# Starts and pass orders that change from column tile to column tile, and three load buffers, in a two-layer decoder trunk

## The chip, the cores and the metric

The kernel runs on one core of a Trainium2 chip. The metric is the time of one execution of the whole program on the device, in microseconds (us). TensorE (PE in the profile) does the matrix products and has two rows there: PE for the matmuls and PEld for the loads of their stationary operand, which overlap them. VectorE is DVE, ScalarE is ACT, GpSimd is POOL, SyncE is SP; SP only issues transfers here.

## What is computed

The input is one sequence of 256 tokens with 1024 features. Two layers follow, and a last norm. Each layer has a half-step SwiGLU, a mixer (a Mamba-2 scan in layer 0, sliding-window attention in layer 1) and another half-step SwiGLU. All is float32.

```python
D_MODEL, SEQ, D_FF = 1024, 256, 2816

def swiglu(h, w_gate, w_up, w_down):
    return (jax.nn.silu(h @ w_gate) * (h @ w_up)) @ w_down

for layer in range(2):
    if layer == 1:
        k_shared, v_shared = shared_kv(x, kv_norm_w, w_k, b_k, w_v, b_v, cos, sin)
    x = x + 0.5 * swiglu(rmsnorm(x, norm_w[layer, 0]), w_gate[layer, 0], w_up[layer, 0], w_down[layer, 0])
    h = rmsnorm(x, norm_w[layer, 1])
    x = x + (mamba2_mixer(h, ...) if layer == 0 else swa_sink_attention(h, k_shared, v_shared, ...))
    x = x + 0.5 * swiglu(rmsnorm(x, norm_w[layer, 2]), w_gate[layer, 1], w_up[layer, 1], w_down[layer, 1])
return rmsnorm(x, final_norm_w)
```

## The kernel before, in words

The activations lie transposed: 8 tiles of 128 features by 256 tokens. Every float32 product is made of three passes of the float32r type: an operand is cut into a rounded high part and the rest, the low part, and the kernel adds high x high, high x low and low x high. The activations' parts stand side by side in `xs` (columns 0 to 255 high, called `xh`; 256 to 511 low, called `xl`). Weights come in units of 128 x 1024; there are 341, in the order that `order()` writes out. A load brings two units (1 MB) into a buffer `raw`, of which there are `RAW`. For each unit ScalarE rounds the high part into a tile `hi` (L144) and VectorE makes the low part `lo` (L155), with six buffers each, four to five units ahead of TensorE. When the second unit of a buffer is cut, `low` issues the next load (L134).

The four SwiGLUs are named (l, i): (0, 0) and (0, 1) in layer 0, (1, 0) and (1, 1) in layer 1. Each goes over 22 column tiles f of 128 hidden features. A tile takes three units: `g` and `u` (gate and up, in `wide`) and, four tiles later, `d` (down, in `rows`). `wide` runs 8 matmuls of 512 columns with `hi` against all of `xs`, and 8 of 256 columns with `lo` against `xh`. They alternate for each k, or, with `by_part`, the 8 wide ones come first and then the 8 narrow ones. `evac` makes the SwiGLU's result and cuts it into `hh` and `hl`, of six buffers each in the pool `op`. `rows` runs 24 matmuls of 256 columns, three for each of 8 output tiles: hi x hh, lo x hh, hi x hl, or with `high_first` hi x hh, hi x hl, lo x hh. Before the change `by_part` (for f > 0) and `high_first` are on where l differs from i, that is in (0, 1) and (1, 0). The output projections of the mixers (`so` in the scan, `ao` in attention) use `rows` without `high_first`. The other units (`dt`, `B`, `C`, `x`, `z`, `qA`, `qB`, `kA`, `kB`) use `unit`: 24 matmuls of 256 columns. The scan and the attention also have small float32 matmuls between units.

The order on each engine is as the code is written; `Slots` only says after which unit a piece of evacuation is issued. A home (the buffer of a tile) is 4096 bytes a partition for `hi` and `lo` and 1024 bytes for `hh` and `hl`, so all homes of a pool start at one place modulo 512 bytes. In the built program that is 160 for `hi`, `lo` and for the key and value operands `xkh` and `xkl`, and 480 for `xs`, `hh` and `hl`.

Of the kernel before, what the change touches and what calls it, by code (L numbers as in the profile page):

```python
# [10 lines left out]
F32R = mybir.dt.float32r  # L11
# [5 lines left out]
P = 128  # L17
T = 256
D = 1024
KT = D // P  # L20
# [11 lines left out]
GROUPS = 4  # L32
EPS = 1e-5
CH = 2
RAW = 4
NEG = -1.0e30


def ffn_order(l, i):
# [32 lines left out]
def order():  # L72
    return ffn_order(0, 0) + ssm_order() + ffn_order(0, 1) + ffn_order(1, 0) + att_order() + ffn_order(1, 1)


ORDER = order()
# [33 lines left out]
class Weights:  # L110
# [27 lines left out]
    def high(self, half=None):  # L138
        u = self.rounded
        c, i = divmod(u, CH)  # L140
        if not half:
            self.hi = self.parts.tile([P, D], F32R, tag="hi", name=f"hi{u}")
        hi, s = self.hi, self.piece(half)
        self.nc.scalar.activation(hi[:, s], self.chunks[c][:, i, s], AF.Copy)  # L144
        if half != 0:
            self.ready[u] = hi
            self.rounded += 1

    def low(self, half=None):
        u = self.cut  # L150
        c, i = divmod(u, CH)
        if not half:
            self.lo = self.parts.tile([P, D], F32R, tag="lo", name=f"lo{u}")
        hi, lo, s = self.ready.get(u, self.hi), self.lo, self.piece(half)
        self.nc.vector.tensor_tensor(lo[:, s], self.chunks[c][:, i, s], hi[:, s].bitcast(F32), ALU.subtract)  # L155
        if half == 0:
            return
        self.ready[u] = (hi, lo)
        self.cut += 1
        if i == CH - 1 or u == NU - 1:  # L160
            del self.chunks[c]
            self.load()

    @staticmethod
    def piece(half):
# [20 lines left out]
class Slots:  # L186
# [11 lines left out]
    def at(self, d, *fs):  # L198
        self.put(d, 0, fs)
# [16 lines left out]
class Trunk:  # L216
    def __init__(self, ctx, tc, a):
# [7 lines left out]
        self.wk = ctx.enter_context(tc.tile_pool(name="work", bufs=2))  # L225
        raw = ctx.enter_context(tc.tile_pool(name="raw", bufs=RAW))
        parts = ctx.enter_context(tc.tile_pool(name="parts", bufs=self.NPART))
# [37 lines left out]
        nc.sync.dma_start(self.sm, a["small"])  # L265
        for _ in range(RAW - 3):
            self.W.load()
# [86 lines left out]
    def wide(self, what, out, by_part=False):  # L354


        hi, lo = self.W.next(what)
        passes = [(k, w, x, n) for k in range(KT) for w, x, n in ((hi, self.xs, 2 * T), (lo, self.xh, T))]
        if by_part:
            passes = passes[0::2] + passes[1::2]  # L360
        for n, (k, w, x, c) in enumerate(passes):
            self.nc.tensor.matmul(  # L362
                out[:, 0:c], w[:, k * P : (k + 1) * P], x[k],
                start=n == 0, stop=n == len(passes) - 1, skip_group_check=True,
            )
        self.tick()
# [2 lines left out]
        self.slots.run()  # L369
        self.W.ahead(self.NPART - 2)  # L370

    def rows(self, units, accs, first, last, done=None, high_first=False):

        nc = self.nc
        for j in range(KT):
            out = accs[j % 4][:, (j // 4) * T : (j // 4) * T + T]
            s = slice(j * P, (j + 1) * P)
            for n, ((hi, lo), hh, hl) in enumerate(units):
                f, e = first and n == 0, last and n == len(units) - 1
                passes = ((hi, hh), (hi, hl), (lo, hh)) if high_first else ((hi, hh), (lo, hh), (hi, hl))  # L380
                for m, (w, x) in enumerate(passes):
                    nc.tensor.matmul(  # L382
                        out, w[:, s], x, start=f and j < 4 and m == 0, stop=e and m == 2, skip_group_check=True
                    )
            if done:
                done(j, out)
# [90 lines left out]
    def ffn(self, l, i, key, nxt):  # L477
        nc, wk = self.nc, self.fw
        self.stage_norm(key)
        accs = self.accs(f"da_{key}")  # L480
        hs = {}

        def evac(f, g, u):
            hh = self.op.tile([P, T], F32R, tag="high", name=f"hh_{key}_{f}")
            hl = self.op.tile([P, T], F32R, tag="low", name=f"hl_{key}_{f}")
            hs[f] = (hh, hl)

            def e0():
                nc.vector.tensor_tensor(g, g, self.rs, ALU.mult)
                nc.scalar.activation(g, g, AF.Silu)  # L490
                nc.vector.tensor_tensor(u, u, self.rs, ALU.mult)

            def e1():
                nc.vector.tensor_tensor(u, u, g, ALU.mult)
                nc.scalar.activation(hh, u, AF.Copy)

            def e2():
                nc.vector.tensor_tensor(hl, u, hh.bitcast(F32), ALU.subtract)

            wait = max(0, 4 - f) if key == "f0" else 2 if f == 0 else 0  # L500
            self.slots.chain(wait, [e0, e1, e2])

        def product(name, f, t):

            b = self.bank(f"{name}_{key}_{f}")
            if self.W.pos == 0:
                self.slots.at(0, lambda: nc.scalar.copy(t, b[:, 0:T]))
                self.unit((name, l, i, f), b[:, 0:T])
                return

            def add():
                nc.scalar.copy(t, b[:, T:])  # L512
                nc.vector.tensor_tensor(t, b[:, 0:T], t, ALU.add)  # L513

            self.slots.at(0, add)
            self.wide((name, l, i, f), b, by_part=l != i and f > 0)

        for f in range(NF):
            g, u = (wk.tile([P, T], F32, tag=n, bufs=4, name=f"{n}s_{key}_{f}") for n in "gu")
            product("g", f, g)  # L520
            evac_now = lambda: evac(f, g, u)
            self.slots.late(0, evac_now)
            product("u", f, u)
            if l == 1 and i == 0 and f == 0:
                self.split_k()
            if l == 1 and i == 0 and f == 5:
                self.shared_k()
            if f >= LAG:
                self.down(l, i, f - LAG, hs, accs)
        for f in range(NF - LAG, NF - 2):  # L530
            self.down(l, i, f, hs, accs)
        self.tail([(("d", l, i, f), *hs.pop(f)) for f in (NF - 2, NF - 1)], accs, nxt)

    def down(self, l, i, f, hs, accs):
        hi_lo = self.W.next(("d", l, i, f))
        hh, hl = hs.pop(f)
        self.rows([(hi_lo, hh, hl)], accs, f == 0, False, high_first=l != i)
        self.tick()

    def tail(self, units, accs, nxt):  # L540
# [519 lines left out]
    def run(self):  # L1060
# [9 lines left out]
        for k in range(KT):  # L1070
            nc.scalar.activation(self.xh[k], self.X[k], AF.Copy, scale=nw(0)(k))
            if k in (1, 5):
                W.high(half=k // 4)
            if k in (2, 6):
                W.low(half=k // 4)
            if k >= 2:
                low(k - 2)
        def square(k):
            self.sq_parts = self.sumsq(self.X[k], k == 0, f"in{k}", k == KT - 1)

        W.high(half=0)
        low(KT - 2)
        W.low(half=0)
        low(KT - 1)
        W.high(half=1)
        W.low(half=1)
# [101 lines left out]
def constants():  # L1188
# [4 lines left out]
    ca = np.zeros((P, NCA), np.float32)  # L1193
    diag = np.where(i[None, :] <= i[:, None], 0.0, NEG)
    prev = np.where(i[None, :] > i[:, None], 0.0, NEG)
    ca[:, 0 : 3 * P] = np.concatenate([diag, prev, diag], 1)
# [38 lines left out]
```

## Time and profile before

| what | us |
|---|---|
| median of 3 runs (lowest, highest) | 1049.97 (1048.2, 1051.52) |
| the profiled execution, and its span | 1048.69, 1046.9 |
| PE busy, share of the span | 1025.2, 98% |
| DVE busy | 775.1, 74% |
| ACT busy | 627.7, 60% |

The span is the time from the first to the last instruction; the 1.8 us beside it are the program's start and end. The stages, by the timeline: SwiGLU (0, 0) from 7 us to 202 us, the scan to 399 us, (0, 1) to 582 us, (1, 0) to 771 us, the attention to 847 us, (1, 1) to 1035 us, then the last norm. A matmul's row in the timeline gives its start and how long it is in flight. Matmuls overlap, so what one costs is the distance from its start to the next one's start, and for a unit the distance from its first start to the next unit's first start.

### The profile page before, as it was taken

How to read it: one execution, taken by the hardware profiler on the slowest of the kernel's cores; microseconds unless marked ns; L12 is line 12 of the kernel's file. 1: busy time of each engine (PE TensorE's matmuls, PEld its weight loads, DVE VectorE, ACT ScalarE, POOL GpSimd, SP SyncE). 2: the span in 40 equal slices, each digit the busy share in tenths (PEclk: the TensorE clock that was granted, in tenths of full speed). 3: DMA queues.
4: the chain of work that ended last, by engine and by line, in shares of the span. 5: the costliest groups of instructions: out<-in, count | busy, mean ns of one | idle time of the engine just before them, and what ended most of it. 6: DMA issues, size and time to landing. Idle time of an engine off the chain costs nothing.

```text
span 1046.9 us, 18340 instructions
## 1 busy us (share of the span) xinstructions
PE 1025.2 (98%) x7290; PEld 948.2 (91%) x7290; DVE 775.1 (74%) x1420; ACT 627.7 (60%) x1106; POOL 79.4 (8%) x122
## 2 busy tenths in 40 slices
PE   8999999999999999999999999999999999999996
PEld 7899999999989898999999899999998888999996
DVE  4766666788999977766667796666689777666664
ACT  6555555669877756555555664555565766555554
POOL 3000000210110112000000200000031020000000
PEclk9999999999999999999999999999999999999998
DMA  8555554546545354555455455554554244555521
GB/s 304 195 201 176 186 200 164 194 171 252 217 156 213 131 201 153 197 201 200 169 203 200 157 211 200 177 209 178 202 202 152 92 161 167 196 186 191 187 101 40
DMA packets 30132, 190.84 MB, mean 182 GB/s; under 512 B 3904, under 2 KB 5728, under 8 KB 8544
## 3 DMA queue, kind: packets, MB, share of 16 engines
q1 hardware_dynamic: 30048, 189.69, 51.0%
q8 instruction: 57, 0.93, 0.4%
q14 instruction: 27, 0.22, 0.1%
HBM read 187.27 MB, written 1.10 MB: 180 GB/s over the span
## 4 chain that ended last, share of the span: by engine, by line
PE 80%; DVE 11%; ACT 3%; DMA 2%; POOL 1%; issue 1%; SPq 0%; ACTq 0%; DVEq 0%; POOLq 0%
PE u_f L362 23%; PE g_f L362 22%; PE da_f L382 22%; PE sa L382 3%; PE sb L349 3%; DVE lo L155 2%; DVE xs L394 2%; DMA csb<-cs_scratch 2%; PE aa L382 1%; PE q L349 1%; DVE xs L601 1%; DVE X L402 1%; DMA raw<-w 1%; DVE E L723 1%; ACT hi L144 1%
## 5 line engine op out<-in xcount | busy, mean ns | idle before, releaser
L155 DVE TENSOR_TENSOR lo<-raw,hi 128x1024 fp32r<-128x1024 f32 (+1 forms) x343 | 415.2, 1214 | 15.0 <-ACT hi L144 15.0
L144 ACT ACTIVATE hi<-raw 128x1024 fp32r<-128x1024 f32 (+1 forms) x343 | 357.3, 1047 | 18.9 <-PE da_f L382 5.1
L362 PE MATMUL u_f<-xs,hi 128*128 128x512 f32 x704 | 218.1, 397 | 0.0
L362 PE MATMUL g_f<-xs,hi 128*128 128x512 f32 x696 | 213.7, 395 | 0.8 <-DVE xs L394 0.8
L382 PE MATMUL da_f<-hh_f,hi 128*128 128x256 f32 x704 | 195.8, 278 | 0.0
L382 PE MATMUL da_f<-hh_f,lo 128*128 128x256 f32 x704 | 195.6, 278 | 0.0
L382 PE MATMUL da_f<-hl_f,hi 128*128 128x256 f32 x704 | 195.6, 278 | 0.0
L362 PEld LDWEIGHTS u_f<-xs,hi 128*128 128x128 f32 x704 | 130.1, 189 | 27.0
L362 PEld LDWEIGHTS g_f<-xs,hi 128*128 128x128 f32 x696 | 127.8, 188 | 27.2 <-DVE xs L394 2.2
L362 PE MATMUL u_f<-xs,lo 128*128 128x256 f32 x704 | 149.4, 280 | 0.0
L362 PE MATMUL g_f<-xs,lo 128*128 128x256 f32 x696 | 148.0, 281 | 0.0
L382 PEld LDWEIGHTS da_f<-hh_f,hi 128*128 128x128 f32 x704 | 132.3, 188 | 1.7
L382 PEld LDWEIGHTS da_f<-hl_f,hi 128*128 128x128 f32 x704 | 132.2, 188 | 0.0
L382 PEld LDWEIGHTS da_f<-hh_f,lo 128*128 128x128 f32 x704 | 132.1, 188 | 0.0
L513 DVE TENSOR_TENSOR gs_f<-g_f,gs_f 128x256 f32<-128x256 f32 x87 | 36.9, 424 | 113.7 <-ACT gs_f L512 113.6
L362 PEld LDWEIGHTS u_f<-xs,lo 128*128 128x128 f32 x704 | 114.1, 189 | 3.7
L362 PEld LDWEIGHTS g_f<-xs,lo 128*128 128x128 f32 x696 | 113.2, 188 | 3.3
L349 PE MATMUL sb<-xs,hi 128*128 128x256 f32 x656 | 108.0, 284 | 0.1
L513 DVE TENSOR_TENSOR us_f<-u_f,us_f 128x256 f32<-128x256 f32 x88 | 37.3, 424 | 88.8 <-ACT us_f L512 88.7
L512 ACT COPY us_f<-u_f 128x256 f32<-128x256 f32 x88 | 32.7, 371 | 111.4 <-PE u_f L362 111.3
L349 PEld LDWEIGHTS sb<-xs,hi 128*128 128x128 f32 x656 | 93.8, 190 | 1.2 <-issue 0.5
L512 ACT COPY gs_f<-g_f 128x256 f32<-128x256 f32 x87 | 32.1, 369 | 89.8 <-PE g_f L362 89.8
(252 smaller groups left out, 1369.4 us busy)
## 6 DMA issues: line engine op xcount, KB each, us to landing
raw<-w SPq DMA_DIRECT2D x168, 1024.0 KB, 4.9
csb<-cs_scratch SPq DMA_DIRECT2D x8, 768.0 KB, 7.0
raw<-w SPq DMA_DIRECT2D x4, 512.0 KB, 8.2
X<-x SPq DMA_DIRECT2D x4, 256.0 KB, 5.9
Q<-r_q SPq DMA_DIRECT2D x32, 32.0 KB, 1.9
out<-o SPq DMA_DIRECT2D x3, 256.0 KB, 2.2
ca<-const_att SPq DMA_DIRECT2D x1, 704.0 KB, 8.2
raw<-w SPq DMA_DIRECT2D x2, 256.0 KB, 5.2
```

Of the source, the lines that this page charges most:

```text
L144: self.nc.scalar.activation(hi[:, s], self.chunks[c][:, i, s], AF.Copy)
L155: self.nc.vector.tensor_tensor(lo[:, s], self.chunks[c][:, i, s], hi[:, s].bitcast(F32), ALU.subtract)
L349: nc.tensor.matmul(out, w[:, k * P : (k + 1) * P], x[k], start=n == 0, stop=n == len(passes) - 1)
L362: self.nc.tensor.matmul(out[:, 0:c], w[:, k * P : (k + 1) * P], x[k], start=n == 0, stop=n == len(passes) - 1, skip_group_check=True,)
L382: nc.tensor.matmul(out, w[:, s], x, start=f and j < 4 and m == 0, stop=e and m == 2, skip_group_check=True)
L394: nc.vector.scalar_tensor_tensor(self.xl[j], self.X[j], wcol(j), self.xh[j].bitcast(F32), ALU.mult, ALU.subtract)
L402: nc.vector.scalar_tensor_tensor(self.X[j], out, scale, self.X[j], ALU.mult, ALU.add)
L512: nc.scalar.copy(t, b[:, T:])
L513: nc.vector.tensor_tensor(t, b[:, 0:T], t, ALU.add)
L601: V.scalar_tensor_tensor(out, u[:, tap : tap + T], self.s("convw", tap * 24 + c), out, ALU.mult, ALU.add)
L723: V.tensor_tensor(f, f, c, ALU.mult)
```

## The change

The homes of `hi` and `lo` grow by 120 columns to 4576 bytes, those of `hh` and `hl` to 1504 bytes. Neither is a multiple of 512, so from buffer to buffer the start moves by 32 bytes modulo 512. On top of that `begin` shifts the data inside the home by 8 columns (32 bytes) times f modulo 16: the weight parts in (0, 0), the operands `hh` and `hl` in (0, 1), the weight parts and, the opposite way, the operands in (1, 1). In (1, 0) nothing is shifted; there the order of passes changes with the tile. `xs` stays where it is. `by_part` is now on in (0, 0), (0, 1) and (1, 1) for f > 0, and in (1, 0) for odd f. `rows` takes its order from `ORDERS`; the first of it, hi x hh, hi x hl, lo x hh, now holds everywhere but in (1, 0), where it is `ORDERS[f % 6]`. In (1, 0) the gate and up units with f % 4 of 2 or 3 have their wide matmul split in two of 256 columns, so 24 matmuls instead of 16. `RAW` falls from 4 to 3.

```diff
-RAW = 4
+RAW = 3
+ROOM = 120
+STEP = 8
+def begin(l, i, f, kind):
+    n = STEP * (f % 16)
+    if (l, i) == (0, 0):
+        return n if kind == "w" else 0
+    if (l, i) == (0, 1):
+        return n if kind == "h" else 0
+    if (l, i) == (1, 1):
+        return n if kind == "w" else ROOM - n
+    return 0
+HH, HL, LH = (0, 0), (0, 1), (1, 0)
+ORDERS = [(HH, HL, LH), (HH, LH, HL), (LH, HH, HL), (HL, HH, LH), (LH, HL, HH), (HL, LH, HH)]
...
-            self.hi = self.parts.tile([P, D], F32R, tag="hi", name=f"hi{u}")
+            w = self.parts.tile([P, D + ROOM], F32R, tag="hi", name=f"hi{u}")
+            self.hi = w[:, self.at(u) : self.at(u) + D]
...
+    def at(u):
+        what = ORDER[u]
+        return begin(*what[1:], "w") if what[0] in ("g", "u", "d") else 0
...
-        passes = [(k, w, x, n) for k in range(KT) for w, x, n in ((hi, self.xs, 2 * T), (lo, self.xh, T))]
+        wide = ((hi, self.xs, 2 * T),)
+        if what[1:3] == (1, 0) and what[3] % 4 > 1:
+            wide = ((hi, self.xh, T), (hi, self.xl, T))
+        passes = [(k, *p) for k in range(KT) for p in wide + ((lo, self.xh, T),)]
         if by_part:
-            passes = passes[0::2] + passes[1::2]
+            passes = [p for q in range(len(wide) + 1) for p in passes[q :: len(wide) + 1]]
...
-                passes = ((hi, hh), (hi, hl), (lo, hh)) if high_first else ((hi, hh), (lo, hh), (hi, hl))
-                for m, (w, x) in enumerate(passes):
+                for m, (wp, hp) in enumerate(order):
...
-            hh = self.op.tile([P, T], F32R, tag="high", name=f"hh_{key}_{f}")
+            o = begin(l, i, f, "h")
+            hh = self.op.tile([P, T + ROOM], F32R, tag="high", name=f"hh_{key}_{f}")[:, o : o + T]
...
-            self.wide((name, l, i, f), b, by_part=l != i and f > 0)
+            self.wide((name, l, i, f), b, by_part=f > 0 and ((l, i) != (1, 0) or f % 2 > 0))
...
-        self.rows([(hi_lo, hh, hl)], accs, f == 0, False, high_first=l != i)
+        self.rows([(hi_lo, hh, hl)], accs, f == 0, False, order=ORDERS[f % 6 if (l, i) == (1, 0) else 0])
```

On TensorE, SwiGLU (0, 0), the gate unit of tile 11 (`g_f_11` is its sum; `xs_84` to `xs_91` are the eight tiles of `xs`), as it stood before:

```order
L362 MATMUL g_f_11_1077<-xs_84,hi_955 128x512
L362 MATMUL g_f_11_1077<-xs_84,lo_983 128x256
L362 MATMUL g_f_11_1077<-xs_85,hi_955 128x512
L362 MATMUL g_f_11_1077<-xs_85,lo_983 128x256
L362 MATMUL g_f_11_1077<-xs_86,hi_955 128x512
L362 MATMUL g_f_11_1077<-xs_86,lo_983 128x256
```

The same place on TensorE now:

```order
L393 MATMUL g_f_11_1075<-xs_84,hi_953 128x512
L393 MATMUL g_f_11_1075<-xs_85,hi_953 128x512
L393 MATMUL g_f_11_1075<-xs_86,hi_953 128x512
L393 MATMUL g_f_11_1075<-xs_87,hi_953 128x512
L393 MATMUL g_f_11_1075<-xs_88,hi_953 128x512
L393 MATMUL g_f_11_1075<-xs_89,hi_953 128x512
L393 MATMUL g_f_11_1075<-xs_90,hi_953 128x512
L393 MATMUL g_f_11_1075<-xs_91,hi_953 128x512
L393 MATMUL g_f_11_1075<-xs_84,lo_981 128x256
L393 MATMUL g_f_11_1075<-xs_85,lo_981 128x256
L393 MATMUL g_f_11_1075<-xs_86,lo_981 128x256
```

The wide matmuls of the eight k now come first, and the narrow ones, which need `lo`, after them; the number of matmuls is the same. The same holds for `u`, and for (1, 1).

On TensorE, SwiGLU (0, 0), the first rows of the down unit of tile 0 (`da_f` are the sums, `hh_f` and `hl_f` the parts of the SwiGLU's result), as it stood before:

```order
L382 MATMUL da_f_205<-hh_f_0_260,hi_393 128x256
L382 MATMUL da_f_205<-hh_f_0_260,lo_421 128x256
L382 MATMUL da_f_205<-hl_f_0_261,hi_393 128x256
L382 MATMUL da_f_206<-hh_f_0_260,hi_393 128x256
L382 MATMUL da_f_206<-hh_f_0_260,lo_421 128x256
L382 MATMUL da_f_206<-hl_f_0_261,hi_393 128x256
```

The same place on TensorE now:

```order
L412 MATMUL da_f_203<-hh_f_0_258,hi_391 128x256
L412 MATMUL da_f_203<-hl_f_0_259,hi_391 128x256
L412 MATMUL da_f_203<-hh_f_0_258,lo_419 128x256
L412 MATMUL da_f_204<-hh_f_0_258,hi_391 128x256
L412 MATMUL da_f_204<-hl_f_0_259,hi_391 128x256
L412 MATMUL da_f_204<-hh_f_0_258,lo_419 128x256
```

hi x hl has moved ahead of lo x hh. In (0, 1) this order stood already.

On TensorE, SwiGLU (1, 0), the first rows of the up unit of tile 2, as they stood before (in the rows of now, x2 is two matmuls of one weight tile, the first with `xh`, the second with `xl`):

```order
L362 MATMUL u_f_2_6924<-xs_84,hi_6785 128x512
L362 MATMUL u_f_2_6924<-xs_85,hi_6785 128x512
L362 MATMUL u_f_2_6924<-xs_86,hi_6785 128x512
L362 MATMUL u_f_2_6924<-xs_87,hi_6785 128x512
L362 MATMUL u_f_2_6924<-xs_88,hi_6785 128x512
L362 MATMUL u_f_2_6924<-xs_89,hi_6785 128x512
L362 MATMUL u_f_2_6924<-xs_90,hi_6785 128x512
L362 MATMUL u_f_2_6924<-xs_91,hi_6785 128x512
L362 MATMUL u_f_2_6924<-xs_84,lo_6811 128x256
L362 MATMUL u_f_2_6924<-xs_85,lo_6811 128x256
L362 MATMUL u_f_2_6924<-xs_86,lo_6811 128x256
```

The same place on TensorE now:

```order
L393 MATMUL u_f_2_6930<-xs_84,hi_6783 128x256 x2
L393 MATMUL u_f_2_6930<-xs_84,lo_6809 128x256
L393 MATMUL u_f_2_6930<-xs_85,hi_6783 128x256 x2
L393 MATMUL u_f_2_6930<-xs_85,lo_6809 128x256
L393 MATMUL u_f_2_6930<-xs_86,hi_6783 128x256 x2
L393 MATMUL u_f_2_6930<-xs_86,lo_6809 128x256
```

The eight matmuls of 512 columns have become sixteen of 256, and `lo` alternates with them again.

On SP the load of the fourth buffer, which stood after `sm` and waited for nothing, is gone from the front. Every later load stands where one stood before, and brings the weights of one buffer earlier in the order.

## Rows read from the trace of the kernel before

**Rows 1.** The page, part 1, busy us (share of the span) x instructions.
```profile
PE 1025.2 (98%) x7290; PEld 948.2 (91%) x7290; DVE 775.1 (74%) x1420; ACT 627.7 (60%) x1106; POOL 79.4 (8%) x122
```
**Rows 2.** Windows: us, busy by engine, (matmuls and others), PEclk, DMA share, GB/s.
```profile
100.00:150.00 50.00, 50.00 (x333) 45.73 (x332) 33.54 (x54) 26.66 (x42) 0.00 (x0) 1.00 0.53 184
...
450.00:500.00 50.00, 50.00 (x341) 45.97 (x340) 33.54 (x55) 27.08 (x44) 0.00 (x0) 1.00 0.54 191
...
700.00:750.00 50.00, 50.00 (x343) 46.06 (x342) 34.07 (x56) 26.72 (x43) 0.00 (x0) 1.00 0.55 192
...
900.00:950.00 50.00, 50.00 (x332) 45.72 (x332) 33.54 (x54) 26.33 (x42) 0.00 (x0) 1.00 0.51 186
```
**Rows 3.** Waits of ACT: who, for whom, us in total, times, longest.
```profile
ACT us_f L512 <- PE u_f L362: 111.3, 80, 2.4
ACT gs_f L512 <- PE g_f L362: 89.8, 73, 4.6
```
**Rows 4.** Timeline of PE in SwiGLU (0, 1): start us, us in flight, instruction.
```profile
480.15 1.99 PE L362 MATMUL g_f<-xs,hi 128*128 128x512 f32 x8
481.98 1.11 PE L362 MATMUL g_f<-xs,lo 128*128 128x256 f32 x8
482.93 2.00 PE L362 MATMUL u_f<-xs,hi 128*128 128x512 f32 x8
484.76 1.07 PE L362 MATMUL u_f<-xs,lo 128*128 128x256 f32 x8
485.67 0.28 PE L382 MATMUL da_f<-hh_f,hi 128*128 128x256 f32 x1
...
488.39 0.62 PE L362 MATMUL g_f<-xs,hi 128*128 128x512 f32 x2
```
**Rows 5.** Timeline of PE in SwiGLU (0, 0).
```profile
105.56 0.40 PE L362 MATMUL g_f<-xs,hi 128*128 128x512 f32 x1
105.79 0.28 PE L362 MATMUL g_f<-xs,lo 128*128 128x256 f32 x1
...
108.38 0.40 PE L362 MATMUL u_f<-xs,hi 128*128 128x512 f32 x1
...
111.21 0.28 PE L382 MATMUL da_f<-hh_f,hi 128*128 128x256 f32 x1
...
114.04 0.40 PE L362 MATMUL g_f<-xs,hi 128*128 128x512 f32 x1
```
**Rows 6.** Timeline of PE around the key units kA and kB in (1, 0).
```profile
619.49 0.28 PE L349 MATMUL kab<-xkh,hi 128*128 128x256 f32 x1
...
625.25 0.28 PE L382 MATMUL da_f<-hh_f,hi 128*128 128x256 f32 x1
...
628.08 0.40 PE L362 MATMUL g_f<-xs,hi 128*128 128x512 f32 x1
```
**Rows 7.** Tile kab and line 382: xcount, ns min/median/max, first and last start.
```profile
L349 PEld LDWEIGHTS kab<-xkh,lo x16: 192/192/193, 619.6 to 625.0; 128*128 128x128 f32 x16
...
L382 PEld LDWEIGHTS da_f<-hh_f,lo x704: 186/188/189, 43.3 to 1034.8; 128*128 128x128 f32 x176
```
**Rows 8.** Line 382 in 816.2:818.9, then in 841.5:844 (attention's output).
```profile
L382 PE MATMUL aa<-oh,lo x8: 280/280/281, 816.2 to 818.7; 128*128 128x256 f32 x8
...
L382 PE MATMUL aa<-oh,lo x8: 276/276/276, 841.5 to 843.9; 128*128 128x256 f32 x8
```
**Rows 9.** Lines of PE in 200:250 (the scan): xcount, busy us, mean ns.
```profile
L349 PE MATMUL sb<-xs,lo 128*128 128x256 f32 x125 | 28.6, 279 | 0.0
```
**Rows 10.** DMA issues: xcount, KB each, median us to landing.
```profile
raw<-w SPq DMA_DIRECT2D x168, 1024.0 KB, 4.9
csb<-cs_scratch SPq DMA_DIRECT2D x8, 768.0 KB, 7.0
```
**Rows 11.** Timeline of SP, then of ACT, at the start.
```profile
14.23 0.33 SPq L134 DMA_DIRECT2D raw<-w  x1
...
19.23 0.33 SPq L134 DMA_DIRECT2D raw<-w  x1
...
22.56 1.07 ACT L144 ACTIVATE hi<-raw 128x1024 fp32r<-128x1024 f32 x1
...
26.29 1.06 ACT L144 ACTIVATE hi<-raw 128x1024 fp32r<-128x1024 f32 x1
```

More of the change, by code (lines that the diff above doesn't have):

```diff
@@ L152, in low @@
         if not half:
-            self.lo = self.parts.tile([P, D], F32R, tag="lo", name=f"lo{u}")
+            w = self.parts.tile([P, D + ROOM], F32R, tag="lo", name=f"lo{u}")
+            self.lo = w[:, self.at(u) : self.at(u) + D]
         hi, lo, s = self.ready.get(u, self.hi), self.lo, self.piece(half)
@@ L162, in low @@
             self.load()
+    @staticmethod
+    def at(u):
+        what = ORDER[u]
+        return begin(*what[1:], "w") if what[0] in ("g", "u", "d") else 0
     @staticmethod
@@ L357, in wide @@
         hi, lo = self.W.next(what)
-        passes = [(k, w, x, n) for k in range(KT) for w, x, n in ((hi, self.xs, 2 * T), (lo, self.xh, T))]
+        wide = ((hi, self.xs, 2 * T),)
+        if what[1:3] == (1, 0) and what[3] % 4 > 1:
+            wide = ((hi, self.xh, T), (hi, self.xl, T))
+        passes = [(k, *p) for k in range(KT) for p in wide + ((lo, self.xh, T),)]
         if by_part:
-            passes = passes[0::2] + passes[1::2]
+            passes = [p for q in range(len(wide) + 1) for p in passes[q :: len(wide) + 1]]
         for n, (k, w, x, c) in enumerate(passes):
+            o = out[:, T:] if x is self.xl else out[:, 0:c]
             self.nc.tensor.matmul(
-                out[:, 0:c], w[:, k * P : (k + 1) * P], x[k],
+                o, w[:, k * P : (k + 1) * P], x[k],
                 start=n == 0, stop=n == len(passes) - 1, skip_group_check=True,
@@ L370, in tick, with rows @@
         self.W.ahead(self.NPART - 2)
-    def rows(self, units, accs, first, last, done=None, high_first=False):
+    def rows(self, units, accs, first, last, done=None, order=ORDERS[0]):
         nc = self.nc
@@ L377, in rows @@
             s = slice(j * P, (j + 1) * P)
-            for n, ((hi, lo), hh, hl) in enumerate(units):
+            for n, (w, hh, hl) in enumerate(units):
                 f, e = first and n == 0, last and n == len(units) - 1
-                passes = ((hi, hh), (hi, hl), (lo, hh)) if high_first else ((hi, hh), (lo, hh), (hi, hl))
-                for m, (w, x) in enumerate(passes):
+                for m, (wp, hp) in enumerate(order):
                     nc.tensor.matmul(
-                        out, w[:, s], x, start=f and j < 4 and m == 0, stop=e and m == 2, skip_group_check=True
+                        out, w[wp][:, s], (hh, hl)[hp],
+                        start=f and j < 4 and m == 0, stop=e and m == 2, skip_group_check=True,
                     )
@@ L483, in evac @@
         def evac(f, g, u):
-            hh = self.op.tile([P, T], F32R, tag="high", name=f"hh_{key}_{f}")
-            hl = self.op.tile([P, T], F32R, tag="low", name=f"hl_{key}_{f}")
+            o = begin(l, i, f, "h")
+            hh = self.op.tile([P, T + ROOM], F32R, tag="high", name=f"hh_{key}_{f}")[:, o : o + T]
+            hl = self.op.tile([P, T + ROOM], F32R, tag="low", name=f"hl_{key}_{f}")[:, o : o + T]
             hs[f] = (hh, hl)
```

## The prediction, made before the changed kernel ran

> **What bounds the kernel now.** I read the busy shares first: TensorE is busy for 1025.2 of 1046.9 us, and PEld for 91% [rows 1]. DVE at 74% and ACT at 60% have room, and ACT waits for TensorE, 111.3 and 89.8 us in its two largest waits [rows 3], not the other way. So the time is the sum of what TensorE's units take, and only a change of their rate counts.
>
> Then the windows of 50 us, to see whether the four SwiGLUs run at one rate. They do not: 333 and 332 matmuls in (0, 0) and (1, 1), 341 and 343 in (0, 1) and (1, 0), all with TensorE busy throughout and the granted clock at 1.00, the upper level of 2.4 GHz [rows 2]. The clock is not the difference. The timeline then prices one column tile, by the distances of starts. In (0, 1), where wide and narrow matmuls stand apart: g 482.93 - 480.15 = 2.78 us, u 485.67 - 482.93 = 2.74, d 488.39 - 485.67 = 2.72, together 8.24 [rows 4]. In (0, 0), where they alternate: 2.82, 2.83 and 2.83, together 8.48 [rows 5].
>
> Per matmul of 256 columns (I call this distance p) d gives 2.72 / 24 = 0.1133 us in (0, 1) and 2.83 / 24 = 0.1179 in (0, 0). A matmul of 512 columns, where eight stand together, takes (481.98 - 480.15) / 8 = 0.2288. The narrow matmuls behind it take 0.95 / 8 = 0.1188 in g, 0.91 / 8 = 0.1138 in u [rows 4].
>
> It would be easy to put the two rates down to the order of passes. Two groups of rows speak against that as the whole cause. The down unit behind the key units stands in the order of (0, 1) and still takes 628.08 - 625.25 = 2.83 us, the slow rate [rows 6]. The attention's output units, in the order of (0, 0), are in flight 280 ns early and 276 ns late in their stage [rows 8], one with the slow rate and one with the fast. So a rate is kept from what went before until something shifts it; the order only decides where it shifts. And a third rate exists: kA and kB take (625.25 - 619.49) / 48 = 0.1200 [rows 6], with weight loads of 192 ns instead of 188 [rows 7]. Their form is that of the scan's units, which run at 279 ns in flight [rows 9], the slow rate; what is special is that their operands and weights start at the same place modulo 512 bytes, where elsewhere 320 bytes lie between. The rows thus show a dependence on starts, for two distances of the sixteen that the change goes through.
>
> **The change part by part.** Nothing is taken off TensorE: every product stays, and 20 units in (1, 0) (10 tiles by two) issue 24 matmuls instead of 16. All of it is therefore a question of p under many starts, which no row shows. The ends are 0.1133 and 0.1200. I take p = 0.1161: 45% at 0.1133, 40% at 0.1179, 15% at 0.1200. The fast rate depends on how a run is entered, and the entries now differ from unit to unit, so I give it less than the four fifths that it has in (0, 1) (u and d are fast, g is not). The wide matmul stays at 0.2288.
>
> A gate or up unit with wide ones first then takes 8 x (0.2288 + p) = 2.76 us, a down unit or a split unit 24 p = 2.79, an alternating one 2.83.
> - (0, 0) and (1, 1): 2.76 + 2.76 + 2.79 = 8.31 against 8.48, 0.17 for 21 tiles, and 0.04 for the down unit of tile 0: -3.6 each, -7.2.
> - (0, 1): 8.31 against 8.24, 22 tiles: +1.5.
> - (1, 0): down units (2.79 - 2.72) x 22 = +1.5; five tiles beyond tile 0 that alternate again, 5.66 against 5.52: +0.7; six with wide ones first: 0; ten split ones, 5.58 against 5.52: +0.6. Together +2.8.
> - The scan's 16 output units, 2.83 to 2.79: -0.6. The attention's 8 run at both rates already: 0.
> - The 49 other units of 24 matmuls in scan and attention keep their order and get other weight starts. They are at the slow rate and small matmuls break them up, so I leave them there: 0, with ends 1176 x (0.1133 - 0.1179) = -5.4 and 1176 x (0.1200 - 0.1179) = +2.5.
> - Three load buffers: 0. A load is issued when a buffer is cut, four units (11 us) before its first part is rounded, and lands after 4.9 us [rows 10]. At the start, the load after the first cut goes out at 14.23 us and the next at 19.23, and they now carry the weights that ACT rounds at 22.56 and 26.29 [rows 11]; 8.3 and 7.1 us are more than 4.9. If that cover fails ACT waits, and TensorE only after the four units that are cut ahead. The ends are 0 and +3.
> - ACT and DVE now write and read at other starts. If that slowed them, DVE's 26% of idle time would hide it: 0.
>
> The sum is -7.2 + 1.5 + 2.8 - 0.6 = -3.5 us. From the profiled execution's 1048.69 this gives 1045.2. That execution was 1.28 below the median of the runs, so against the median of 1049.97 the forecast is 1046.5.
>
> The ends by the same sum: with p = 0.1133 throughout, -12.2 - 1.0 - 0.4 - 1.8 = -15.4, and -21 with the other units. With p = 0.1179, -4.3 + 3.0 + 4.7 = +3.4. With p = 0.1200, -0.8 + 4.8 + 7.0 + 0.8 = +11.8, and +14 with the other units. The change is worth nothing at p = 0.1170.
>
> **The rivals.**
> Order alone decides (0.15). Then starts are free, and what (0, 1) shows carries over: (0, 0) and (1, 1) gain 0.24 x 42 = 10.1, the scan's output units 16 x 0.11 = 1.8, and (1, 0) loses 0.7 for the alternating tiles, 0.7 for the five split ones that alternate, and 11 x 0.11 = 1.2 for the down units whose order is a rotation of the old one. That is -9.3: 1040.7. For it speaks the regularity of rows 4 and 5; against it rows 6 to 8. The Trainium skill stands on its side: "SBUF — State Buffer", section "SBUF: two separate sides", says that TensorE has ports of its own and never waits on anyone, and "TensorE: Matmul & The Clock Gate" gives it one read port for the moving operand and another for the weights, so that no two starts could collide. The trace does not agree, by the 0.1200 of kA and kB.
>
> The fast rate is lost, and the result is slower (0.23). It is one mechanism: in (0, 1) the fast rate holds through u and d because each unit enters as the one before left; with starts that move by 32 bytes from tile to tile every unit enters anew and falls to 0.1179, as the unit behind kA and kB did. Only wide ones first remain as a gain. +3.4: 1053.4. It decides from p above 0.1170, which is when fewer than about a fifth of the runs are fast.
>
> Most starts are as bad as that of kA and kB (0.11): p near 0.1200, +11.8 to +14, 1062 to 1064. For it: 0.1200 is what one of the two distances known gives. Against it: the equal start may be the worst of the sixteen.
>
> Three buffers run dry in the scan (0.04). There eight transfers of 768 KB take 7.0 us each ahead of a load of 4.9 [rows 10], 11.9 us against 11.3 of cover. If each miss reached TensorE with 0.6 to 1 us, the 4.8 to 8 would turn the forecast into 1051 to 1054.5. Against it: parts are cut four units ahead.
>
> **How the numbers follow.** The forecast, mixed rates with p between 0.1150 and 0.1170, has 0.47 and reaches from 1041 to 1050. A measurement here tells 0.3% (3.15 us) from no change, so faster is below 1046.8, slower above 1053.1. Faster: order alone, 0.15, and somewhat over half of the forecast, 0.27: 0.42. Same: the rest of the forecast, 0.20, 0.08 of the lost fast rate, where p is under 0.1178, and half of the dry buffers, 0.02: 0.30. Slower: 0.15 of the lost fast rate, the bad starts 0.11 and the other half, 0.02: 0.28. The range for 8 in 10 goes from 1037, which leaves out most of the way to p = 0.1133 everywhere, to 1057, which leaves out the bad starts.
>
> **What would show it.** In the timeline, gate and up units of (0, 0) and (1, 1) at 2.74 to 2.79 us instead of 2.82; the windows there at 335 to 341 matmuls in 50 us. Down units of the four SwiGLUs no longer at one rate but between 2.72 and 2.88, and tiles with the same start at the same rate. (0, 1) slower by 1 to 3 us as a stage, with no edit to its order; if it keeps its 183 us, starts don't matter and the first rival holds. PEld rows of 192 ns where the third rate stands. Waits of ACT on a load beyond the start would show the buffers. The forecast is wrong if TensorE gets idle time that it had not, if wide matmuls leave 0.2288, or if p falls below 0.1133 or rises above 0.1200 under some start: then the ends were no ends.

## The result, and the profile after

The changed kernel took 1056.87 us (median of 3 runs, 1056.78 to 1057.33) against 1049.97: a ratio of 1.0068 with a 95% interval of 1.0042 to 1.0093. It is slower by 6.9 us, where 1046.5 was forecast. The profiled execution took 1056.78 us, its span 1055.0 against 1046.9.

The page first, part 1, in the form of [rows 1]:

```profile
PE 1032.3 (98%) x7450; PEld 961.9 (91%) x7450; DVE 775.0 (73%) x1420; ACT 628.1 (60%) x1106; POOL 79.6 (8%) x122
```

PE is busy for 7.1 us more, and DVE and ACT for as long as before, to 0.4 us. Nothing new is waited for either: the two large waits of ACT for TensorE answer to [rows 3] within 4 us, and the loads land as in [rows 10], after 4.9 us, those of the scan after 7.4 us, 0.4 later.

```profile
ACT us_f L544 <- PE u_f L393: 111.9, 79, 2.4
ACT gs_f L544 <- PE g_f L393: 93.8, 73, 4.7
```

So TensorE does its matmuls more slowly. The windows of [rows 2], now (us; busy by engine with the number of instructions: PE, PEld, DVE, ACT, POOL; PEclk; DMA share; GB/s):

```profile
100.00:150.00 50.00, 50.00 (x333) 45.73 (x332) 33.54 (x54) 26.52 (x42) 0.00 (x0) 1.00 0.55 184
...
450.00:500.00 50.00, 50.00 (x333) 45.81 (x333) 33.50 (x54) 26.68 (x42) 0.00 (x0) 1.00 0.55 190
700.00:750.00 50.00, 50.00 (x395) 48.61 (x394) 32.63 (x55) 25.79 (x43) 0.00 (x0) 1.00 0.55 190
900.00:950.00 50.00, 50.00 (x332) 45.72 (x331) 33.54 (x54) 26.68 (x42) 0.00 (x0) 1.00 0.54 184
```

The first and last hold the 333 and 332 matmuls that they had, at the same clock, 1.00: the new order of passes brought nothing there. The second fell from 341 to 333, with no edit to its order of passes. (The third holds split matmuls and can't be compared by number.) The timeline of one tile in (0, 1), start and time in flight, answers to [rows 4]:

```profile
481.35 2.01 PE L393 MATMUL g_f<-xs,hi 128*128 128x512 f32 x8
483.20 1.11 PE L393 MATMUL g_f<-xs,lo 128*128 128x256 f32 x8
484.15 2.03 PE L393 MATMUL u_f<-xs,hi 128*128 128x512 f32 x8
...
486.96 0.28 PE L412 MATMUL da_f<-hh_f,hi 128*128 128x256 f32 x1
...
489.81 2.00 PE L393 MATMUL g_f<-xs,hi 128*128 128x512 f32 x8
```

g takes 2.80, u 2.81 and d 2.85 us, together 8.46 against 8.24. And one in (0, 0), against 8.48 in [rows 5]:

```profile
105.29 2.03 PE L393 MATMUL g_f<-xs,hi 128*128 128x512 f32 x8
107.16 1.11 PE L393 MATMUL g_f<-xs,lo 128*128 128x256 f32 x8
108.10 2.03 PE L393 MATMUL u_f<-xs,hi 128*128 128x512 f32 x8
...
110.93 0.28 PE L412 MATMUL da_f<-hh_f,hi 128*128 128x256 f32 x1
...
113.76 0.63 PE L393 MATMUL g_f<-xs,hi 128*128 128x512 f32 x2
```

2.81, 2.83 and 2.83, together 8.47: the order of (0, 1) without its rate. Eight wide matmuls take 1.87 us here and 1.85 above, 0.2338 and 0.2313 each where [rows 4] had 0.2288; so the wide ones became dearer too. From the first start of a stage's first gate unit to the last start of its last down unit, (0, 0) is 0.4 us longer (all of it in the first four tiles; from tile 4 on it is 0.3 shorter), (1, 1) 0.9 shorter, (0, 1) 4.3 longer, (1, 0) 4.7 longer, and the rest of the program 0.4 shorter: together the 8.1 us of the spans.

### The profile page after: what moved, and what is told of

It reads as the page before. It is cut to its first block, busy times and chain, and to the rows that moved or that the text cites. A ratio compares the mean times of both kernels' runs of the same rounds, so it can differ in the third digit from the quotient of the medians.

```text
span 1055.0 us, 18647 instructions
## 1 busy us (share of the span) xinstructions
PE 1032.3 (98%) x7450; PEld 961.9 (91%) x7450; DVE 775.0 (73%) x1420; ACT 628.1 (60%) x1106; POOL 79.6 (8%) x122
## 4 chain that ended last, share of the span: by engine, by line
PE 80%; DVE 11%; ACT 3%; DMA 2%; POOL 1%; issue 1%; SPq 0%; DVEq 0%; POOLq 0%
PE u_f L393 23%; PE da_f L412 23%; PE g_f L393 22%; PE sa L412 3%; PE sb L376 3%; DVE lo L177 2%; DMA csb<-cs_scratch 2%; PE aa L412 2%; DVE xs L425 1%; PE q L376 1%; DVE xs L633 1%; ACT hi L165 1%; DMA raw<-w 1%; DVE E L755 1%; ACT E L750 1%
## 5 line engine op out<-in xcount | busy, mean ns | idle before, releaser
L412 PE MATMUL da_f<-hl_f,hi 128*128 128x256 f32 x704 | 198.0, 281 | 0.0
L412 PE MATMUL da_f<-hh_f,lo 128*128 128x256 f32 x704 | 197.8, 281 | 0.0
L393 PE MATMUL u_f<-xs,hi 128*128 128x512 f32 (+1 forms) x784 | 190.8, 373 | 0.0
L393 PE MATMUL g_f<-xs,hi 128*128 128x512 f32 (+1 forms) x776 | 187.2, 371 | 0.7 <-DVE xs L425 0.7
L393 PEld LDWEIGHTS u_f<-xs,hi 128*128 128x128 f32 x784 | 134.8, 188 | 21.8
L393 PEld LDWEIGHTS g_f<-xs,hi 128*128 128x128 f32 x776 | 133.0, 188 | 22.5 <-DVE xs L425 1.7
L393 PE MATMUL u_f<-xs,lo 128*128 128x256 f32 x704 | 113.4, 281 | 0.0
L393 PE MATMUL g_f<-xs,lo 128*128 128x256 f32 x696 | 111.0, 280 | 0.0
L393 PEld LDWEIGHTS u_f<-xs,lo 128*128 128x128 f32 x704 | 101.1, 189 | 6.1
L393 PEld LDWEIGHTS g_f<-xs,lo 128*128 128x128 f32 x696 | 99.4, 188 | 6.1
```

Of the source, the lines that this page charges most:

```text
L393: self.nc.tensor.matmul(o, w[:, k * P : (k + 1) * P], x[k], start=n == 0, stop=n == len(passes) - 1, skip_group_check=True,)
L412: nc.tensor.matmul(out, w[wp][:, s], (hh, hl)[hp], start=f and j < 4 and m == 0, stop=e and m == 2, skip_group_check=True,)
```

## The experiments

### Orders, starts and buffers apart

Four kernels shared the runs of the kernel before, whose median was 1047.51 us. The first is the kernel before with the pass orders of (0, 1) everywhere (the default of `high_first` in `rows` is true as well):

```diff
-            self.wide((name, l, i, f), b, by_part=l != i and f > 0)
+            self.wide((name, l, i, f), b, by_part=f > 0)
...
-        self.rows([(hi_lo, hh, hl)], accs, f == 0, False, high_first=l != i)
+        self.rows([(hi_lo, hh, hl)], accs, f == 0, False, high_first=True)
```

> The kernel before with wide ones first (for f > 0) and high x high, high x low, low x high in all four SwiGLUs and both output projections; homes, starts and four load buffers as before. If the moved starts caused the loss (theory S), this kernel shows what the orders alone are worth: tiles of (0, 0) and (1, 1) at 8.24 us like those of (0, 1), 42 x 0.24 = 10 us less, about 1040. If the orders themselves lost the time (theory O), it is no faster than before: 1050 or more.

1038.70 us, ratio 0.9919 (0.9904 to 0.9934). All four SwiGLUs run at the rate of (0, 1) now; the timeline of (0, 0):

```profile
105.48 2.00 PE L362 MATMUL u_f<-xs,hi 128*128 128x512 f32 x8
...
108.23 0.28 PE L382 MATMUL da_f<-hh_f,hi 128*128 128x256 f32 x1
...
110.95 1.99 PE L362 MATMUL g_f<-xs,hi 128*128 128x512 f32 x8
...
113.72 2.00 PE L362 MATMUL u_f<-xs,hi 128*128 128x512 f32 x8
```

u 2.75, d 2.72, g 2.77 us: 8.24. The order alone is worth 8.8 us.

The second is the kernel before with three load buffers:

```diff
-RAW = 4
+RAW = 3
```

> The kernel before with three load buffers and nothing else changed. Theories S and O: 1050, within 1 us. Theory B (the third rival of the prediction, buffers that run dry): 1053 or more, with waits of ACT on loads in the scan.

1048.90 us, 1.0013 (1.0003 to 1.0023). The buffers cost 1.4 us (0.13%) and are not the cause.

The third has the changed kernel's homes, shifts and three buffers, with the pass orders of the kernel before:

```diff
-        if what[1:3] == (1, 0) and what[3] % 4 > 1:
+        if False:
...
-    def rows(self, units, accs, first, last, done=None, order=ORDERS[0]):
+    def rows(self, units, accs, first, last, done=None, order=ORDERS[1]):
...
-            self.wide((name, l, i, f), b, by_part=f > 0 and ((l, i) != (1, 0) or f % 2 > 0))
+            self.wide((name, l, i, f), b, by_part=l != i and f > 0)
...
-        self.rows([(hi_lo, hh, hl)], accs, f == 0, False, order=ORDERS[f % 6 if (l, i) == (1, 0) else 0])
+        self.rows([(hi_lo, hh, hl)], accs, f == 0, False, order=ORDERS[0 if l != i else 1])
```

> The changed kernel with the orders of the kernel before, so only homes, starts and three load buffers are new. Theory S: (0, 1) and (1, 0) lose their fast rate, 44 x (8.45 - 8.24) = 9 us, and (0, 0) and (1, 1) stay at about 8.48: 1057 to 1063, slower than the changed kernel. Theory O: 1050, as before.

1054.54 us, 1.0071 (1.0054 to 1.0088): the whole loss, with none of the new orders. It is less than the 1057 to 1063 expected: in the profiled executions (0, 1) and (1, 0) lose 4.3 and 4.0 us, near the 9, but (0, 0) and (1, 1) become 2.0 and 1.0 us shorter. The fourth has the changed kernel's orders, split and three buffers, with homes of 4096 and 1024 bytes and no shift:

```diff
-ROOM = 120
+ROOM = 0
...
 def begin(l, i, f, kind):
+    return 0
```

> The changed kernel with homes and starts as before: all its orders, the split units in (1, 0) and three load buffers. Theory S: the gain of the orders less what the mixture in (1, 0) costs at fixed starts (2 to 5 us): 1042 to 1046. Theory O: the 1057 of the changed kernel.

1040.57 us, 0.9938 (0.9923 to 0.9952), a little below the 1042 expected: the mixture of orders costs (1, 0) 2.6 us, and (0, 0) and (1, 1) gain 11.5. From here to the changed kernel only the starts differ: 1.0068 less 0.9938 is 0.0130, 13.6 us. The orders, with three buffers, gain 0.6% where the starts stay, and nothing where they move (1.0068 against 1.0071).

### Which starts are slow

The next two kernels take the best orders, three buffers and homes that are multiples of 512 bytes, and hold the weights' start constant for half a stage (tiles 0 to 10, then 11 to 21): eight starts in one kernel, 32 bytes apart. Only the weights of g, u and d move, `xs`, `hh` and `hl` do not. The second kernel goes on with eight more, 256 bytes further. I name a start by its distance: start of the moving operand less start of the weights, modulo 256 bytes. Before the change it is 64 (480 - 160 = 320), and 0 in kA and kB.

```diff
-ROOM = 120
+ROOM = 128
 def begin(l, i, f, kind):
-    n = STEP * (f % 16)
...
+    if kind == "w":
+        return STEP * STARTS[2 * (2 * l + i) + f // 11]
+    return 0
+STARTS = [0, 1, 2, 3, 4, 5, 6, 7]
...
```

> Orders of the first experiment everywhere, three load buffers, homes of the weight parts of 4608 bytes (a multiple of 512), those of the operands as before. Each half of each SwiGLU (tiles 0 to 10, tiles 11 to 21) has one start of its weight parts, moved by 0, 32, 64, ... 224 bytes in order of time, so that the distance of moving operand and weights modulo 512 is 320, 288, 256, 224, 192, 160, 128, 96 and stays over eleven tiles. Theory D (the distance sets the rate): 8.24 us per tile in the first half of (0, 0), and different, constant values in the others, up to 8.5, the order of halves in no relation to time. Theory C (only the change of start from tile to tile loses the fast rate, by a new entry): 8.24 us per tile in all halves but for their first one or two tiles.

> The same with starts moved by 256 to 480 bytes: distances 64, 32, 0, 480, 448, 416, 384, 352 in order of time. Theory D: different constant values, and distance 0 (first half of (0, 1)) near the 0.1200 of kA and kB, 8.4 to 8.5 us per tile. Theory C: 8.24 in all halves.

1055.56 and 1054.29 us in one run each, beside 1047.70 for the kernel before. A down unit runs four tiles late, so the first four of a half stage stand beside gate and up units that have already moved on. The means of g, u and d in the first kernel, in ns, are therefore taken over tiles 5 to 10 and 16 to 21 and the down units between them, where all three have the start of the half stage:

| distance | half stage | g | u | d | tile |
|---|---|---|---|---|---|
| 64 | (0, 0) first | 2772 | 2741 | 2721 | 8234 |
| 32 | (0, 0) second | 2808 | 2805 | 2800 | 8413 |
| 0 | (0, 1) first | 2793 | 2793 | 2880 | 8466 |
| 224 | (0, 1) second | 2813 | 2813 | 2840 | 8467 |
| 192 | (1, 0) first | 2774 | 2773 | 2723 | 8270 |
| 160 | (1, 0) second | 2822 | 2810 | 2815 | 8447 |
| 128 | (1, 1) first | 2801 | 2799 | 2849 | 8449 |
| 96 | (1, 1) second | 2827 | 2827 | 2880 | 8533 |

The second kernel gives the same tile times in the same half stages within 3 ns, so a start 256 bytes further is the same start, and only modulo 256 counts. A constant start is not enough to be fast; the distance decides. At distance 0, d takes 2.88 us, 24 x 0.1200: the 0.1200 of kA and kB. The mean of the eight is 8.41 us, a little less than the 8.43 to 8.47 of the changed kernel's stages (from tile 4 on), which go through all eight. The clock is not the difference: from 27 us to the end of (1, 1) it is granted at 1.00 in both kernels, as before the change, but for short stretches in the scan.

Two distances have the fast rate. At 192, d runs at 24 x 0.1133 as at 64, and only the wide matmuls are dearer there, (650.45 - 648.59) / 8 = 0.2325 where 64 has 0.2288; a tile takes 8.27 us:

```profile
648.59 2.02 PE L388 MATMUL g_f<-xs,hi 128*128 128x512 f32 x8
650.45 1.07 PE L388 MATMUL g_f<-xs,lo 128*128 128x256 f32 x8
651.36 2.02 PE L388 MATMUL u_f<-xs,hi 128*128 128x512 f32 x8
...
654.14 0.28 PE L407 MATMUL da_f<-hh_f,hi 128*128 128x256 f32 x1
...
656.86 2.02 PE L388 MATMUL g_f<-xs,hi 128*128 128x512 f32 x8
```

The four down units at 192 that run after g and u have moved on to 160 take 2.83 us. So one distance can have two rates, by what runs around it. The timeline at distance 64, then at 96:

```profile
70.97 1.99 PE L388 MATMUL g_f<-xs,hi 128*128 128x512 f32 x8
...
73.74 2.00 PE L388 MATMUL u_f<-xs,hi 128*128 128x512 f32 x8
...
76.48 0.28 PE L407 MATMUL da_f<-hh_f,hi 128*128 128x256 f32 x1
...
79.20 1.07 PE L388 MATMUL g_f<-xs,hi 128*128 128x512 f32 x4
...
979.67 2.03 PE L388 MATMUL g_f<-xs,hi 128*128 128x512 f32 x8
...
982.50 2.03 PE L388 MATMUL u_f<-xs,hi 128*128 128x512 f32 x8
...
985.33 0.28 PE L407 MATMUL da_f<-hh_f,hi 128*128 128x256 f32 x1
...
988.21 1.09 PE L388 MATMUL g_f<-xs,hi 128*128 128x512 f32 x4
```

8.23 and 8.54 us, and in the second all three units are longer. Whether the fast distance has a width was asked next, with the step at 4 bytes:

```diff
-STEP = 8
+STEP = 1
...
-    if kind == "w":
-        return STEP * STARTS[2 * (2 * l + i) + f // 11]
-    return 0
+    if kind != "w":
+        return 0
+    return STARTS[2 * (2 * l + i) + f // 11]
...
-STARTS = [0, 1, 2, 3, 4, 5, 6, 7]
+STARTS = [60, 61, 62, 63, 1, 2, 3, 4]
```

> The sweep of starts with steps of 4 bytes around the best distance: modulo 256 bytes the distances are 80, 76, 72, 68, 60, 56, 52 and 48 in order of time, each over eleven tiles. Theory D16 (the unit of the effect is a line of 16 or 32 bytes): 68, 72 and 76 run as 64 or as 80, in steps; at most 8.24 to 8.5 us per tile. Theory P (a smooth phase): per-tile times between 8.24 and 8.5 that rise on both sides of 64, or fall below 8.24 on one side.

1058.03 us in one run beside 1048.05. Distances 80, 76, 72, 68, 60, 56, 52 and 48 give 8.408, 8.453, 8.420, 8.467, 8.446, 8.468, 8.630 and 8.400 us a tile. Four bytes to either side of 64 lose 0.2 us: no theory had put the fast place so narrow. At 52 d takes 24 x 0.1217, above the upper end of the prediction. The odd multiples of 16, with 96 and 64 again in other stages than before:

```diff
-STARTS = [60, 61, 62, 63, 1, 2, 3, 4]
+STARTS = [56, 12, 52, 44, 36, 28, 20, 0]
```

> Distances modulo 256 of 96, 16, 112, 144, 176, 208, 240 and 64 in order of time. Theory D (distance, not stage or time): 96 now in the first half of (0, 0) has 8.53 us per tile as it had in the last half of the last sweep, 64 in the last half of (1, 1) has 8.24; the odd multiples of 16 lie between 8.24 and 8.55. If the stage decided, the halves would keep their last values instead, 8.24 first and 8.53 last.

1056.42 us in one run, beside the same 1048.05. 96, now in (0, 0), gives 8.533 again: the stage is not what made it slow. 16, 112, 144, 176, 208 and 240 give 8.373, 8.533, 8.520, 8.457, 8.466 and 8.460. But 64, now in the second half of (1, 1), gives 8.340 where 8.24 was expected:

```profile
981.96 2.00 PE L388 MATMUL g_f<-xs,hi 128*128 128x512 f32 x8
...
984.70 1.99 PE L388 MATMUL u_f<-xs,hi 128*128 128x512 f32 x8
...
987.47 0.28 PE L407 MATMUL da_f<-hh_f,hi 128*128 128x256 f32 x1
...
990.30 1.08 PE L388 MATMUL g_f<-xs,hi 128*128 128x512 f32 x4
```

g 2.74, u 2.77, d 2.83: g and u have exchanged the times of [rows 4], and d is slow. The same distance and the same order thus have two cycles that each last, and what came before picks one.

This limits what the sweeps say of the other distances. Eleven of them stand in the first half of a SwiGLU, entered from its start, as 64 is in the order-only kernel, where all four stages are fast; of these 192 has the fast rate, and 0, 52, 60, 72, 80, 96, 112, 128, 176 and 240 have not. The other ten were entered from another distance only, so that they have no fast rate under any entry is not shown.

To see what d does beside other g and u, weights and operands were moved together, so that d stays at 64 while g and u go through the eight distances of the first sweep:

```diff
-ROOM = 128
+ROOM = 64
...
-    if kind != "w":
-        return 0
     return STARTS[2 * (2 * l + i) + f // 11]
...
-STARTS = [56, 12, 52, 44, 36, 28, 20, 0]
+STARTS = [0, 8, 16, 24, 32, 40, 48, 56]
...
-            hh = self.op.tile([P, T], F32R, tag="high", name=f"hh_{key}_{f}")[:, o : o + T]
-            hl = self.op.tile([P, T], F32R, tag="low", name=f"hl_{key}_{f}")[:, o : o + T]
+            hh = self.op.tile([P, T + ROOM], F32R, tag="high", name=f"hh_{key}_{f}")[:, o : o + T]
+            hl = self.op.tile([P, T + ROOM], F32R, tag="low", name=f"hl_{key}_{f}")[:, o : o + T]
```

> As the first sweep (weight starts moved by 0, 32, ... 224 bytes by halves), but the SwiGLU's operands move by the same amount, so that in the down units the distance is 64 modulo 256 in every half while gate and up units run through all eight. Theory D: down units at 2.72 us in every half, gate and up units as in the first sweep. If the start itself counts and not the distance, down units vary from 2.72 to 2.88 as in the first sweep. If a unit keeps the rate of the one before (history), down units are at 2.83 in all halves but the first.

1054.31 us in one run. d takes 2.721 us in the first half stage and 2.824 to 2.830 in the other seven; the first sweep had 2.72 to 2.88. That the distance of 64 makes d fast everywhere (theory D) has failed; the times of its last alternative, that a unit keeps the rate of the one before, are what came. Its reason does not hold everywhere: in (1, 0) first the narrow matmuls of u, at 192, take 0.1140, and d right behind them is slow. The timeline of (0, 1) first, where g and u are at 0:

```profile
421.41 2.00 PE L386 MATMUL g_f<-xs,hi 128*128 128x512 f32 x8
...
424.20 2.00 PE L386 MATMUL u_f<-xs,hi 128*128 128x512 f32 x8
...
426.99 0.28 PE L405 MATMUL da_f<-hh_f,hi 128*128 128x256 f32 x1
...
429.82 1.55 PE L386 MATMUL g_f<-xs,hi 128*128 128x512 f32 x6
```

d is 2.83 us, 24 x 0.1179, not the 2.88 of distance 0 nor the 2.72 of the fast rate. So for d it is the distance and not the place of the weights that sets the possible rates: seven places give one time here, where seven distances gave six. At 64 there are two, 0.1133 and 0.1178, and the units before pick one. For g and u place and distance were not parted, since `xs` never moved.

### The homes without the shift

The changed kernel with its homes of 4576 and 1504 bytes, best orders, three buffers, and no shift by f:

```diff
 def begin(l, i, f, kind):
+    return 0
...
-        if what[1:3] == (1, 0) and what[3] % 4 > 1:
+        if False:
...
-            self.wide((name, l, i, f), b, by_part=f > 0 and ((l, i) != (1, 0) or f % 2 > 0))
+            self.wide((name, l, i, f), b, by_part=f > 0)
...
-        self.rows([(hi_lo, hh, hl)], accs, f == 0, False, order=ORDERS[f % 6 if (l, i) == (1, 0) else 0])
+        self.rows([(hi_lo, hh, hl)], accs, f == 0, False, order=ORDERS[0])
```

> The wide homes of the change (4576 and 1504 bytes, so starts differ by 32 bytes from buffer to buffer) with nothing shifted inside them, three load buffers and the best order everywhere. Theory D: the starts differ from unit to unit although nothing is shifted on purpose, and the loss is nearly that of the changed kernel: 1050 to 1057. If only the shift with the tile mattered: 1039 to 1041.

1056.85 us in one run, beside 1048.05, with 333 to 335 matmuls in each window. The drift from buffer to buffer by itself brings the whole loss.

### Keeping the rate, or never having it

If runs of 256 columns keep the rate they enter with, splitting all wide matmuls freezes it. One kernel is the order-only kernel with every wide matmul of the SwiGLUs split from tile 4 on, but not in tile 6 of (1, 0), the first behind kA and kB; the other splits from tile 1 on (its condition is `what[3] > 0`). Distance, orders and buffers stay.

```diff
+        wide = ((hi, self.xs, 2 * T),)
+        if what[3] > 3 and what[1:] != (1, 0, 6):
+            wide = ((hi, self.xh, T), (hi, self.xl, T))
```

> The first experiment's kernel (best orders, homes and four buffers as before) with the wide matmuls of gate and up units split in two of 256 columns from tile 4 on, but for tile 6 of (1, 0), behind the key units. Theory H (a run keeps its rate, fast or slow, until something shifts it; a group of eight wide matmuls shifts it, matmuls of 256 columns don't): the tiles before hand over the fast rate, and all 72 matmuls of a split tile keep it, 72 x 0.1133 = 8.16 us against 8.24, for 71 tiles 5.6 us less than the first experiment, 0.987 of before, about 1034. Theory M (24 more matmuls per tile cost their overhead, at the mixed rate 0.116): 8.35 us per tile, 1047.

> The same with the split from tile 1 on, so that no group of wide matmuls stands between a stage's start, with its small float32 matmuls, and its end. Theory H: each SwiGLU stays at the rate that chance gives it at its first tiles, 8.16 or 8.48 us per tile, the same for all tiles from 4 on, at least one of the four slow, and (1, 0) slow behind the key units: 1039 to 1060, slower than the other kernel of this call. If a split unit is fast by itself: 1034 or less.

Beside 1047.65 us for the kernel before, the first took 1032.16 (1030.68 to 1032.73), ratio 0.9847 (0.9832 to 0.9861), the second 1059.03 (1057.09 to 1059.46), ratio 1.0099 (1.0082 to 1.0116). The timeline of (0, 0) in the first, then in the second:

```profile
76.97 1.98 PE L366 MATMUL g_f<-xs,hi 128*128 128x256 f32 x16
...
79.69 1.98 PE L366 MATMUL u_f<-xs,hi 128*128 128x256 f32 x16
...
82.42 0.28 PE L386 MATMUL da_f<-hh_f,hi 128*128 128x256 f32 x1
```
```profile
71.82 2.04 PE L366 MATMUL g_f<-xs,hi 128*128 128x256 f32 x16
...
74.65 2.05 PE L366 MATMUL u_f<-xs,hi 128*128 128x256 f32 x16
...
77.48 0.28 PE L386 MATMUL da_f<-hh_f,hi 128*128 128x256 f32 x1
...
80.30 2.04 PE L366 MATMUL g_f<-xs,hi 128*128 128x256 f32 x16
```

2.72 us a unit in one, 24 x 0.1133, and 2.83 in the other, 24 x 0.1178, for the same 72 matmuls of a tile (16 more than with whole wide ones), and so in all four SwiGLUs. The kernels differ in tiles 1 to 3 of each SwiGLU and tile 6 of (1, 0) alone, and are 27 us apart. Those few tiles with wide matmuls bring TensorE into the fast rate, and in the first kernel it leaves it once: the down unit behind kA and kB takes 2.84 us, and that of tile 6, behind whole wide matmuls, 2.72 again.

```profile
615.76 0.28 PE L386 MATMUL da_f<-hh_f,hi 128*128 128x256 f32 x1
...
618.60 2.00 PE L366 MATMUL g_f<-xs,hi 128*128 128x512 f32 x8
...
621.38 2.00 PE L366 MATMUL u_f<-xs,hi 128*128 128x512 f32 x8
...
624.12 0.28 PE L386 MATMUL da_f<-hh_f,hi 128*128 128x256 f32 x1
...
626.84 1.98 PE L366 MATMUL g_f<-xs,hi 128*128 128x256 f32 x16
```

The first kernel is the fastest of all here.

## Why the prediction was wrong

The step that failed is "I take p = 0.1161: 45% at 0.1133, 40% at 0.1179, 15% at 0.1200". It treated the fast rate as one that close to half of the matmuls would have. The sweeps show it at two of 22 distances, 64 and 192; at the 20 others tiles take 8.37 to 8.63 us, and 64 was what homes of 4096 and 1024 bytes happened to give. In the changed kernel as built, 520 of the 5096 matmuls of the four SwiGLUs are at 64 and 600 at 192, and no unit has all its matmuls at one distance. Its mean p is 0.1183.

- (0, 0) and (1, 1), forecast at -7.2: -0.5. The orders would have brought it at distance 64 (order_only); the starts took it.
- (0, 1), forecast at +1.5: +4.3, and (1, 0), forecast at +2.8: +4.7. The signs were right; the mean tile went to 8.43 in (0, 1) and 8.47 in (1, 0).
- "The wide matmul stays at 0.2288" failed too: with the wide ones first, 0.229 stands at distance 64 alone, and 0.230 to 0.236 at the others. In (0, 0), (0, 1) and (1, 1) of the changed kernel it is 0.2323 on the mean: 0.0035 x 8 for 126 gate and up units is +3.5.
- Together: between its ends of +3.4 (p = 0.1179) and +11.8 (p = 0.1200) the prediction's sum gives +5.0 for 0.1183, and with the +3.5 of the wide ones +8.5, where the spans differ by 8.1 and the medians by 6.9.
- Three buffers at 0, with ends 0 and +3: +1.4 for the whole edit, inside. ACT and DVE at 0: right.
- "kA and kB special by their starts": right, d at distance 0 takes their rate. In the changed kernel they are at distances of 128 to 192 and take (629.55 - 623.86) / 48 = 0.1185, with weight loads of 188 ns instead of the 192 of [rows 7]:

```profile
623.86 0.28 PE L376 MATMUL kab<-xkh,hi 128*128 128x256 f32 x1
...
629.55 0.28 PE L412 MATMUL da_f<-hh_f,hi 128*128 128x256 f32 x1
```
```profile
L376 PEld LDWEIGHTS kab<-xkh,lo x16: 187/188/193, 624.0 to 629.3; 128*128 128x128 f32 x16
```

The rival that came true is the lost fast rate, given 0.23. Its +3.4 is short by the wide matmuls and by a p a little above 0.1179. Its reason was half right. It said that every unit "enters anew" at starts that change; in the sweeps the start is constant for eleven tiles, and at 20 of 22 distances they are slow all the same. There the distance, entered as it was, has no fast rate; the entry was seen to pick where there are two, at 64 and 192.

The first rival, order alone, priced the orders well: -9.3, where the same orders without the starts (orders_as_changed) gave -6.9 with the +1.4 of three buffers in it. It failed on "starts are free". The Trainium skill stood on its side ("SBUF — State Buffer", section "SBUF: two separate sides": TensorE never waits on anyone). Taken to hold for TensorE's own two reads against each other, as the prediction took it, this disagrees with the runs: 8.23 or 8.53 us for the same matmuls by the distance of their starts. That it is the two reads that collide is not shown.

What the prediction had right was read in [rows 6] and [rows 8]: a rate is kept from what went before. The two split kernels show it, and it fits the down unit behind kA and kB in [rows 6], slow at distance 64. In the order of (0, 1), a group of eight wide matmuls stands between a slow narrow group in g and a fast one in u, each time; there the rate is shifted.

What stays open is what in the units before picks the rate where the distance changes between units, what makes the other distances slow inside the chip, why the period is 256 bytes, and why at 192 the matmuls of 256 columns are fast (0.1133 in d, 0.1140 in g and u) while the wide ones take 0.2327.

## What to carry to other kernels

Where TensorE is busy throughout, take the distance from the start of the moving operand to the start of the weights, modulo 256 bytes, as a parameter to sweep (64 was the best of 22 here, 192 the second), and keep homes at multiples of 256 so that it is the same in each buffer. Compare starts of matmuls, not the order of passes alone: one order gave 8.24 or 8.46 us a tile here by the homes. Where two rates are seen for the same code, look at how the first units enter; here a few tiles at the front of the stages decided 27 us.

## What the runs showed that was not expected

- The fast distance is narrower than 4 bytes to either side: 8.23 us a tile at 64, 8.47 at 68 and 8.45 at 60; and it repeats after 256 bytes within 3 ns. A second one stands 128 bytes further, at 192, with 8.27.
- At one distance, with one order, 24 matmuls take 2.72 or 2.83 us for a whole stage, by what ran before.
- At the fast rate a matmul of 512 columns with its weights (0.2288) is dearer than two of 256 with the same weights loaded twice (2 x 0.1133 = 0.2267).
